# A two-layer hybrid transformer on one core: the first projections fed by adaLN sums in another order, with unread products, split sums and a fixed order of three engines

## The chip, the cores and the metric

The kernel runs on one core of one Trainium2 chip. A core has a matrix engine (TensorE, "PE"; its weight loads are listed as "PEld"), a vector engine (VectorE, "DVE"), a scalar engine (ScalarE, "ACT"), a general engine (GpSimd, "POOL") and a queue engine (SyncE, "SP") that here only issues DMAs. Each engine works through its own queue in order and waits there for semaphores. The metric is the device time of one execution in microseconds (us), the median of several runs.

## The reference

Two residual blocks on a latent sequence `x` (256 x 1024) and a context `ctx` (256 x 1024). Layer 0 mixes by a chunked retention, layer 1 by neighbourhood attention; each is followed by an MLP. What matters here is the start of layer 0: six modulation vectors from one matrix product with `silu(c)` ("ada"), the affine of x and ctx with the first two, and the projection of the result.

```python
silu_c = jax.nn.silu(c)
silu_cc = jax.nn.silu(c_ctx)
for i in range(DEPTH):
    mod = (silu_c @ ada_w[i] + ada_b[i])[:, None, :]
    mod_c = silu_cc @ ada_w[i] + ada_b[i]
    sh1, sc1, g1, sh2, sc2, g2 = jnp.split(mod, 6, axis=-1)
    sh1c, sc1c, g1c, sh2c, sc2c, g2c = jnp.split(mod_c, 6, axis=-1)

    h = x * (1.0 + sc1) + sh1
    hc = ctx * (1.0 + sc1c) + sh1c
    if i % N_MIXERS == 0:
        y, yc = retention_mixer(h, hc, ret_w_in[j], ret_w_o[j], ret_decay[j],
                                ang_row, ang_col, not last)
    ...
    x = layer_norm(DN_ALPHA * x + g1 * y, ln_g[i, 0], ln_b[i, 0])
    ...
```

In the retention mixer `p = h @ w_in` gives q, k, v and a gate for four heads; q and k have 256 columns a head, v and the gate 512.

## The kernel before

**Products in two parts.** All large products are made from float32 values that are split in a high part (rounded to TensorE's fp32r format) and a low part (the difference). `split` makes the high part on ACT and the low part on DVE; `mm3` makes a product from three passes: high by high, high by low, low by high. Activations for the projections stand transposed in `hTh` and `hTl`: eight chunks of 128 features by 512 tokens (256 latent, then 256 context).

**Weights.** `specs` lists all weight blocks in the order of use. `fetch` loads one (`raw`, four buffers), ACT makes `hi`, DVE makes `lo` (five buffers each); `take` hands out the next blocks and fetches ahead.

**The first quarters.** Head 0's q (256 columns) and v (512 columns) are accumulated over eight chunks in six PSUM banks, `pq` (two) and `pv` (four), while ada arrives. The work goes in four quarters of 256 features. `quarter_loads` loads for a quarter ada's columns of the shift (s = 0) and of the scale (s = 1), each in two blocks of 512 rows (`kh`), and then the quarter's columns of x and ctx into `RR`. `quarter_rows` makes ada's sums: `ada_mm` puts 128 columns in each of four 32-row strips of one bank, per input chunk k four small products; `ada_row` adds the bias rows `brows` and stores the row; `ada_columns` turns the row into columns with a product by `sel` and writes `mods[0, 0]` (adding 1 to the scale). `chunk` transposes a feature chunk of x and ctx into one bank; `modulate_chunk` applies the affine, DVE to the latent half and ACT to the context half, and splits the result. `quarter_q` and `quarter_v` are the products, 6 and 12 passes a chunk, so 36 a quarter. `quarter_weights` takes the quarter's two weight blocks.

**The start.** `crow` gathers c, c_ctx and the four norms' rows ln_g and ln_b; one transpose turns them into columns, from which `scol` (silu), `cT` (silu repeated, the stationary operand of ada's sums) and `lnT` come. `lns` is a scaled copy of the norm rows in DRAM, which the layer norms read much later. `cst` holds the constants: identity, `sel`, rotation tables.

**Order.** `InOrder` wraps each engine; where `.on` is set, the instructions of this engine keep the order of the program, else a planner orders them at build time by priority and estimated time. Before, SP is in program order through the quarters, TensorE is ordered by the planner, and ACT and DVE are in program order only around `make_strip`, which makes the four decay strips from exponentials of `dt` (`strip_tables`): none in quarter 0, strip 0 in quarter 1, strip 1 in quarter 2, strips 2 and 3 in quarter 3.

**Behind the quarters.** x and ctx are scaled by ALPHA; head 0's q is rotated (`rotate`, from `pq`), v is copied and split (`evac_v`, from `pv`), k is projected (`proj_T`), then come the gates, the masked scores and the outputs. In the background (`bg`) the rest of ada streams in (`rawa`) and is weighed on DVE.

Of the kernel before, what the change touches and what calls it, by code (L numbers as in the profile page):

```python
# [17 lines left out]
P = 128  # L18
# [21 lines left out]
def make_consts():  # L40
# [14 lines left out]
    add("sel", sel)  # L55
    inv = f(1.0) / (f(10000.0) ** (np.arange(0, 128, 2, dtype=f) / f(128.0)))
# [8 lines left out]
    add("pad", np.zeros((P, -sum(q.shape[1] for q in parts) % LINE)))  # L65
# [39 lines left out]
def kernel(  # L105
# [169 lines left out]

    def lows(n=100):
# [14 lines left out]
    cst = cpool.tile([P, CONSTS.shape[1]], F32, tag="cst", name="cst")  # L291
# [3 lines left out]
    sp.dma_start(out=cst[:], in_=consts)  # L295
    act.dma_start(out=crow[16:48, :], in_=ln_g.rearrange("l i (k p) -> (l i k) p", p=P))
    act.dma_start(out=crow[48:80, :], in_=ln_b.rearrange("l i (k p) -> (l i k) p", p=P))

    def cv(name, p0=0, p1=P):
        o, w = CONST_COLS[name]  # L300
        return cst[p0:p1, o : o + w]
# [6 lines left out]
    pc = bank("pc")  # L308
    pe.transpose(pc[:, 0:80], crow[0:80, :], ident[0:80, 0:80])
    act.activation(out=scol[:].rearrange("p a k -> p (a k)"), in_=pc[:, 0:16], func=AF.Silu)  # L310
    for t in range(2):
        dve.tensor_copy(
            out=cT[:, :, :, t], in_=scol[:, t, :].unsqueeze(2).broadcast_to([P, KC, 16])
        )
    dve.tensor_copy(out=lnT[:].rearrange("p a b c k -> p (a b c k)"), in_=pc[:, 16:80])


    lns = dram.tile([64, P], F32, tag="lns", name="lns")
    lsc = scr("lsc")
    pool.tensor_scalar_mul(out=lsc[0:80, :P], in0=crow[0:80, :], scalar1=ALPHA)  # L320
    act.dma_start(out=lns[:], in_=lsc[16:80, :P])

    mhalf = small(cpool, 1, "mhalf", name="mhalf")
    dve.memset(mhalf[:], -0.5)

    onecol = small(cpool, 33, "onecol", name="onecol")
    lgn = cpool.tile([P, 2, 8], F32, tag="lgn", name="lgn")
    lgm = small(cpool, 4, "lgm", name="lgm")
# [60 lines left out]
    def ada_quarter_load(i, ss):  # L389

        raws = []
        for kh in range(2):
            raw = slot(ss[kh], [P, 2, 4, 256], F32, "rawq")
            for s in range(2):
                w_ap = ada_w[0][512 * kh : 512 * kh + 512, s * D + 256 * i : s * D + 256 * i + 256]
                sp.dma_start(out=raw[:, s], in_=w_ap.rearrange("(k p) n -> p k n", p=P))
            raws.append(raw)
# [291 lines left out]
    pv = [bank("pv") for _ in range(4)]  # L689
    AQ = ((S_GS, S_SH), (S_SL, S_VH))  # L690

    def quarter_loads(i):
        raws = ada_quarter_load(i, AQ[i % 2])
        for a, src in enumerate((x, ctx_in)):
            cols = slice(256 * i, 256 * i + 256)
            sp.dma_start(out=RR[a][:, :, cols], in_=src[0][:, cols].rearrange("(t p) c -> p t c", p=P))
        return raws

    def quarter_ada(pr, raws, kh):
        for k in range(4 * kh, 4 * kh + 4):  # L700
            ada_mm(pr, k, P, lambda j: raws[kh][:, j // 2, k - 4 * kh, (j % 2) * P : (j % 2 + 1) * P])
# [45 lines left out]
    raws = quarter_loads(0)  # L747
    brows = slot(S_T1, [P, 4, P], F32, "brows")
    for j in range(4):
        act.dma_start(  # L750
            out=brows[32 * j : 32 * j + 32],
            in_=bass.AP(
                ada_b.tensor,
                ada_b.offset + (j // 2) * D + (j % 2) * P,
                [[0, 32], [256, 4], [1, P]],
            ),
        )
    def quarter_rows(i, raws):
        pr = bank("pada")
        for kh in range(2):  # L760
            quarter_ada(pr, raws, kh)
        return pr, ada_row(pr, brows[:, i], P)

    def quarter_weights(i):
        return take(1, 2)[0], take(1, 1 if i < 3 else WB)[0]
# [7 lines left out]

    def modulate_chunk(k, pt):
        m = mods[0, 0]
        tmp = scr("aff")
        dve.tensor_scalar(
# [26 lines left out]
    for i in range(4):  # L804
# [16 lines left out]
        if i < 3:  # L821
            wq, wv = wnext
# [1046 lines left out]
```

## Time and profile before

| | us |
|---|---|
| median of three runs | 1231.76 (1231.55 to 1233.69) |
| the profiled execution | 1231.76 |
| its span, first to last instruction | 1230.0 |

All waits within the first 130 us that are above 5 us, by engine and what it waited for: DVE's `row` for TensorE's `pada` 24.7 us in four waits; ACT's `aff` for DVE's `aff` 21.6 us in five; ACT's `hi` for the weights' DMA 13.1 us in three. TensorE itself waited 5.0 us for the first rows of `crow` and 3.3 us for `rawq`.

How to read the rows: in the timeline a row has the start, the length, the engine, the line (a helper records every operation here, so all have the same line and are told apart by their tiles), the operation, out<-in, the count that was merged, and in brackets the idle time before it and what ended it. A float32 matmul stands as two records; a transpose as one. In the table of stretches the columns are the stretch, its length, the busy time and number of instructions of PE, PEld, DVE, ACT and POOL, the granted TensorE clock, the busy share of the DMA engines and GB/s.

### The profile page before, as it was taken

The page shows a single profiled execution, that of the slowest core. Times are in us where ns is not written, and L with a number is a line of the kernel's source. Part 1 is how long each engine was busy: PE and PEld are TensorE (multiplying, and loading weights), DVE is VectorE, ACT ScalarE, POOL GpSimd, SP SyncE. Part 2 cuts the span into 40 slices and gives each one's busy share as a digit, 9 for nine tenths or more (in the row PEclk, how much of TensorE's full clock was granted, in tenths as well). Part 3 has the DMA queues.
Part 4 walks back from the last instruction along what each step waited for, and adds up shares of the span by engine and source line. Part 5 has one row for each costly group of instructions (what it writes and reads, how often), then busy time and mean ns, then how long its engine had stood idle before and what let it go on. Part 6 is the DMA issues. An engine that isn't in the chain of part 4 may idle for free.

```text
span 1230.0 us, 17924 instructions
## 1 busy us (share of the span) xinstructions
PE 1198.3 (97%) x7069; PEld 1000.7 (81%) x7069; DVE 809.0 (66%) x1256; ACT 477.5 (39%) x795; POOL 167.4 (14%) x198
## 2 busy tenths in 40 slices
PE   6999999999999999999999999999999989999996
PEld 4777888888888888888888888788887867999885
DVE  2597857777585476667766664467575678776445
ACT  2462232323223245442113341146465565655340
POOL 2004401420340140000120000131111110000001
PEclk9999999999999999999999999999999999999998
DMA  9665443375543224326656656336345643565660
GB/s 310 224 210 193 142 133 107 120 245 124 149 154 105 75 69 138 111 90 205 197 164 213 193 182 215 126 87 184 88 138 158 187 140 108 179 211 187 223 206 35
DMA packets 140516, 194.53 MB, mean 158 GB/s; under 512 B 22440, under 2 KB 84112, under 8 KB 140432
## 3 DMA queue, kind: packets, MB, share of 16 engines
q1 hardware_dynamic: 135440, 180.86, 46.4%
q0 software_dynamic: 3264, 9.46, 3.0%
q10 hardware_dynamic: 1728, 3.07, 0.8%
q8 instruction: 55, 0.90, 0.3%
q14 instruction: 29, 0.24, 0.1%
HBM read 188.53 MB, written 5.75 MB: 158 GB/s over the span
## 4 chain that ended last, share of the span: by engine, by line
PE 85%; DVE 6%; ACT 4%; DMA 2%; issue 1%; POOL 1%; SPq 0%; DVEq 0%; POOLq 0%; ACTq 0%
PE p L84 41%; PE pq L84 7%; PE pv L84 7%; PE pw L84 6%; PE pg L84 6%; PE pn L84 4%; PE pnv L84 3%; PE pada L84 2%; PE po L84 2%; ACT s L84 2%; DVE lo L84 1%; DMA rawa<-in_ada_w_dram 1%; PE pnw L84 1%; PE ppt L84 1%; PE pS L84 1%
## 5 line engine op out<-in xcount | busy, mean ns | idle before, releaser
L84 DVE TENSOR_TENSOR lo<-raw,hi 128x1024 fp32r<-128x1024 f32 (+1 forms) x228 | 277.2, 1226 | 158.5 <-ACT hi L84 158.4
L84 ACT CAST hi<-raw 128x1024 fp32r<-128x1024 f32 (+1 forms) x228 | 234.1, 1036 | 353.5 <-PE p L84 183.5
L84 PE MATMUL p<-hi,hid 128*128 128x512 f32 (+1 forms) x832 | 242.4, 374 | 0.0
L84 PEld LDWEIGHTS p<-hi,hid 128*128 128x128 f32 x832 | 152.2, 188 | 28.7 <-issue 1.2
L84 PE MATMUL p<-hTh,lo 128*128 128x256 f32 (+1 forms) x512 | 169.6, 331 | 0.8 <-DVE lo L84 0.8
L84 PE MATMUL p<-hTh,hi 128*128 128x256 f32 (+1 forms) x512 | 169.9, 332 | 0.0
L84 PE MATMUL p<-hTl,hi 128*128 128x256 f32 (+1 forms) x512 | 169.3, 331 | 0.0
L84 PE MATMUL p<-lo,hid 128*128 128x512 f32 (+1 forms) x416 | 155.3, 373 | 0.0
L84 POOL TENSOR_TENSOR R<-R,acc 128x512 f32<-128x512 f32 x40 | 65.9, 1657 | 298.9 <-DVE acc L84 298.7
L84 PEld LDWEIGHTS p<-hTh,lo 128*128 128x128 f32 x512 | 98.0, 191 | 9.7 <-DVE lo L84 1.0
L84 PEld LDWEIGHTS p<-hTh,hi 128*128 128x128 f32 x512 | 98.0, 191 | 9.5 <-issue 0.8
L84 PEld LDWEIGHTS p<-hTl,hi 128*128 128x128 f32 x512 | 98.0, 191 | 8.7
L84 DVE SCALAR_TENSOR_TENSOR acc<-rawa,scol,acc 128x1024 f32<-128x1024 f32 x49 | 62.2, 1282 | 46.7 <-DMA rawa<-in_ada_w_dram 46.6
L84 PEld LDWEIGHTS p<-lo,hid 128*128 128x128 f32 x416 | 78.4, 188 | 13.5
L84 DVE SCALAR_TENSOR_TENSOR strips<-rawa,scol,strips 128x512 f32<-128x512 f32 x84 | 70.0, 885 | 4.0 <-DMA rawa<-in_ada_w_dram 4.0
L84 ACT CAST hid<-r 128x256 fp32r<-128x256 f32 (+1 forms) x64 | 32.0, 500 | 83.6 <-DVE r L84 83.6
L84 POOL TENSOR_SCALAR rstd<-mv 128x1 f32<-128x1 f32 x28 | 10.5, 376 | 366.7 <-DVE mv L84 366.7
L84 ACT ACTIVATE s<-s,mn 128x512 f32<-128x512 f32 x64 | 45.5, 712 | 32.3 <-DVE mn L84 32.3
L84 DVE TENSOR_TENSOR hid<-r,hid 128x256 fp32r<-128x256 f32 (+1 forms) x64 | 34.6, 541 | 29.5 <-ACT hid L84 29.4
L84 PE MATMUL pq<-hTh,hi 128*128 128x512 f32 x128 | 50.4, 397 | 1.8 <-ACT hTh L84 1.8
L84 PE MATMUL pw<-hi,oh 128*128 128x512 f32 x128 | 51.2, 400 | 0.0
L84 PE MATMUL pg<-hi,hTh 128*128 128x512 f32 x128 | 51.0, 398 | 0.0
(191 smaller groups left out, 2248.0 us busy)
## 6 DMA issues: line engine op xcount, KB each, us to landing
raw<-in_mlp_w_dram SPq DMA_DIRECT2D x128, 512.0 KB
rawa<-in_ada_w_dram SPq DMA_DIRECT2D x80, 512.0 KB
raw<-in_ret_w_in_dram SPq DMA_DIRECT2D x46, 512.0 KB
raw<-in_nat_w_in_dram SPq DMA_DIRECT2D x24, 512.0 KB
rawq<-in_ada_w_dram SPq DMA_DIRECT2D x16, 512.0 KB
raw<-in_ret_w_o_dram SPq DMA_DIRECT2D x16, 512.0 KB
bias<-rpb_rows POOLq DMA_DIRECT2D x16, 256.0 KB, 4.2
raw<-in_nat_w_o_dram SPq DMA_DIRECT2D x8, 512.0 KB
```

The source lines that it names most:

```text
L84: r = f(*args, **kwargs)
```

## The change

**Start.** The constants are loaded in two parts: `cst0` (identity, `sel` and a new `sel2`, 140 columns) at once, the rest in quarter 0. `crow` gathers c, c_ctx and ada's bias for the first two vectors; the norm rows come in quarter 1 (`ln_rows`, on ACT's queue), their transpose, `lnT` and `lns` in quarter 3 (`ln_columns`; `lns` goes from ACT's queue to POOL's). `brows` and its four DMAs are gone: the bias stands in columns (`bcol`, with the 1 of the scale) and is added where `mods` is written.

**Loads.** x's and ctx's first quarter goes on ACT's queue, later ones on SP's ahead of ada's blocks. The blocks come in the order s = 0 (both `kh`), then s = 1. The first two weight blocks are loaded ahead of the second quarter; `load` leaves the making of their parts to two functions, `high` and `low`, which are called one chunk at a time.

**Order.** From `first_columns` to the end of the quarters ACT, DVE and TensorE keep the program's order.

**Sums.** `quarter_sums` makes the sums of one s from 16 matmuls of 128 columns: even and odd input chunks in different strips, which `sel2` adds up when the row becomes columns. Their number for a quarter stays (32).

**First quarter.** The transposes of chunks 0 and 1, by kind (latent, context) into two banks each, stand between the third and the fourth ada block; 4, 3 and 6 short products of a constant tile (`turn_over`), whose result nothing reads, stand ahead of the last sums, between them and the columns, and behind the columns. `modulate_kinds` writes the high part of each kind straight from PSUM (ACT latent, DVE context), then the other way round a full copy, and the low part as the difference. `first_products` orders the 18 passes of chunk 0 by the parts as they come.

**Later quarters.** The sums stand in halves between v's products of the quarter before; the second half of the sums' bank takes the context's transposes. `modulate_chunk` now makes the high part on DVE and the full copy on ACT. The ALPHA scaling and three weight blocks come ahead of quarter 3's last products.

```diff
+    def load():
+        src, k, ncol = specs[len(units)]
+        raw = rawp.tile([P, k, ncol], F32, tag="raw", name=nm("raw"))
+        sp.dma_start(out=raw[:], in_=src.rearrange("(k p) n -> p k n", p=P))
+        ...
+        def high(i):
+            act.copy(out=hi[:, i], in_=raw[:, i])
+        def low(i):
+            dve.tensor_sub(out=lo[:, i], in0=raw[:, i], in1=hi[:, i].bitcast(F32))
+        return high, low
...
-    sp.dma_start(out=cst[:], in_=consts)
-    act.dma_start(out=crow[16:48, :], in_=ln_g.rearrange("l i (k p) -> (l i k) p", p=P))
-    act.dma_start(out=crow[48:80, :], in_=ln_b.rearrange("l i (k p) -> (l i k) p", p=P))
+    act.dma_start(out=crow[16:32, :], in_=ada_b[0][0 : 2 * D].rearrange("(r p) -> r p", p=P))
+    act.dma_start(out=cst0[:], in_=consts[:, 0:NC0])
...
+    def ln_rows():
+        rows = scr("rows")[:, :P]
+        act.dma_start(out=rows[0:32, :], in_=ln_g.rearrange("l i (k p) -> (l i k) p", p=P))
+        act.dma_start(out=rows[32:64, :], in_=ln_b.rearrange("l i (k p) -> (l i k) p", p=P))
+        return rows
...
+    def turn_over(n):
+        for _ in range(n):
+            pe.matmul(pq[0][:, :256], lhsT=still[:, :P], rhs=still[:, :256], start=True, stop=True)
...
+    def quarter_sums(pr, raws, s, ks):
+        for k in ks:
+            lhsT = cT[:, k, :, :].rearrange("p a t -> p (a t)")
+            for half in range(2):
+                j = 2 * (k % 2) + half
+                pe.matmul(
+                    pr[32 * j : 32 * j + 32, tsl(s)],
+                    lhsT=lhsT,
+                    rhs=raws[k // 4][:, s, k % 4, tsl(half)],
+                    ...
+    def quarter_columns(pr, row, c0):
+        for s in range(2):
+            pe.matmul(
+                pr[:, 4 * s : 4 * s + 4], lhsT=row[:, tsl(s)], rhs=cv("sel2"), start=True, stop=True
+            )
+        dve.tensor_add(out=mods[0, 0][:, :, c0 : c0 + 2, :], ...
...
     def modulate_chunk(k, pt):
...
-        split(tmp[:], hTh[:, k, :], hTl[:, k, :])
+        tmp = scr("aff")
+        for e, dst in ((dve, hTh[:, k, :]), (act, tmp)):
+            for a in range(2):
+                modulated(e, dst[:, KINDS[a]], pt[:, KINDS[a]], k, a)
+        dve.tensor_sub(out=hTl[:, k, :], in0=tmp[:], in1=hTh[:, k, :].bitcast(F32))
+
+    def modulate_kinds(k, pts, between=lambda: None):
+        tmp = scr("aff")
+        for e, a in ((act, 0), (dve, 1)):
+            modulated(e, hTh[:, k, KINDS[a]], pts[a], k, a)
+        between()
+        for e, a in ((act, 1), (dve, 0)):
+            modulated(e, tmp[:, KINDS[a]], pts[a], k, a)
+        dve.tensor_sub(out=hTl[:, k, :], in0=tmp[:], in1=hTh[:, k, :].bitcast(F32))
...
+    quarter_x(0, act)
+    raws = ada_quarter_load(0, AQ[0])
+    wq_parts, wv_parts = load(), load()
+    raws1 = quarter_loads(1)
+    for e in (act, dve, pe):
+        e.on = True
+    pr = bank("pada")
+    first_columns()
+    quarter_sums(pr, raws, 0, range(KC))
+    quarter_sums(pr, raws, 1, range(0, 4))
+    pts = [chunk_kinds(k) for k in range(2)]
+    turn_over(4)
+    quarter_sums(pr, raws, 1, range(4, KC))
+    row = quarter_row(pr)
+    turn_over(3)
+    quarter_columns(pr, row, 0)
+    turn_over(6)
+    (qhigh, qlow), (vhigh, vlow) = wq_parts, wv_parts
+    qhigh(0)
+    modulate_kinds(0, pts[0], lambda: qlow(0))
+    vhigh(0)
+    vlow(0)
+    qhigh(1)
+    modulate_kinds(1, pts[1])
+    qlow(1)
+    vhigh(1)
+    vlow(1)
...
     for i in range(4):
         k = 2 * i
-        quarter_q(k, 0, wq)
+        wq, wv = take(2, 0)
         if i < 3:
-            pr, row = quarter_rows(i + 1, raws)
-        quarter_v(k, 0, wv)
+            wq_parts, wv_parts = load(), load()
+        if i == 0:
+            tabs = strip_tables()
+            sp.dma_start(out=cst1[:], in_=consts[:, NC0:])
+        if i < 2:
+            raws2 = quarter_loads(i + 2)
+        if i == 0:
+            first_products(wq, wv)
+        else:
+            quarter_q(k, 0, wq)
+            modulate_chunk(k + 1, chunk(k + 1))
+            quarter_v(k, 0, wv)
...
         quarter_q(k + 1, 1, wq)
+        if i == 3:
+            ln_columns(rows)
+            take(0, 3)
+            for a in range(2):
+                dve.tensor_scalar_mul(out=RR[a][:], in0=RR[a][:], scalar1=ALPHA)
+            quarter_v(k + 1, 1, wv)
+        else:
+            pr = bank("pada")
+            quarter_sums(pr, raws, 0, range(KC))
+            quarter_v(k + 1, 1, wv, range(2))
+            if i:
+                both(wv_parts)
+            pts = chunk_kinds(k + 2, pr)
+            quarter_sums(pr, raws, 1, range(KC))
+            row = quarter_row(pr)
+            quarter_v(k + 1, 1, wv, (2,))
+            quarter_columns(pr, row, k + 2)
+            modulate_kinds(k + 2, pts)
+            quarter_v(k + 1, 1, wv, (3,))
+            if i == 0:
+                both(wv_parts)
+            if i == 1:
+                rows = ln_rows()
+            raws = raws2
         for h in ((), (0,), (1,), (2, 3))[i]:
             make_strip(h, *tabs)
-        act.on = dve.on = False
+    act.on = dve.on = False
```

More of the change, by code (lines that the diff above doesn't have):

```diff
@@ L64, in make_consts @@
         add("sin" + nm, np.sin(ang) * sg)
-    add("pad", np.zeros((P, -sum(q.shape[1] for q in parts) % LINE)))
     base = np.concatenate(parts, axis=1)
@@ new lines, in both @@
+    def both(parts):
+        for k in range(2):
+            for f in parts:
+                f(k)
+    quarter_x(0, act)
[11 more added lines that the diff above has]
+    quarter_sums(pr, raws, 1, range(4, KC))
```

170 lines of the change are left out of this document (94 added, 76 removed).

## The prediction, made before any run of the changed kernel

> **What bounds the kernel now.** I read the page first, then busy time by stretches, then the timeline of the first 80 us, because the change lies there.
>
> ```profile
> span 1230.0 us, 17924 instructions
> PE 1198.3 (97%) x7069; PEld 1000.7 (81%) x7069; DVE 809.0 (66%) x1256; ACT 477.5 (39%) x795; POOL 167.4 (14%) x198
> ```
> ```profile
> 6.00:18.60 12.60, 7.35 (x74) 4.99 (x74) 2.23 (x8) 2.18 (x5) 0.00 (x0) 1.00 1.09 339
> 62.00:70.00 8.00, 8.00 (x36) 6.50 (x36) 7.86 (x14) 8.00 (x15) 0.00 (x0) 1.00 0.63 211
> ```
>
> TensorE has work in 97% of the span, so the time is TensorE's queue plus its gaps. The stretch from 6 to 18.6 us is the largest gap: TensorE is busy for 7.35 of 12.60 us while the DMA engines are full (share 1.09, 339 GB/s). The profiled execution is itself the median run, 1231.76 us: its span of 1230.0 and 1.76 around it. My sum is made against that.
>
> The head, before the first product, reads so:
>
> ```profile
> 1.35 0.33 ACTq L84 DMA_DIRECT2D crow<-in_ln_g_dram  x1
> 1.61 3.63 SPq L84 DMA_DIRECT2D rawq<-in_ada_w_dram  x4
> 1.71 0.43 ACTq L84 DMA_DIRECT2D crow<-in_ln_b_dram  x1
> ...
> 11.23 0.19 PEld L84 LDWEIGHTS pada<-rawq,cT 128*32 128x32 f32 x4 [0.58 <-DMA rawq<-in_ada_w_dram]
> ...
> 12.70 1.92 PE L84 MATMUL pada<-rawq,cT 128*32 128x128 f32 x28 [0.83 <-DMA rawq<-in_ada_w_dram]
> 14.56 1.12 PE L84 MATMUL pt<-cst,R 128*128 128x128 f32 x4
> 14.67 0.29 DVE L84 TENSOR_TENSOR row<-pada,brows 128x128 f32<-128x128 f32 x1 [8.56 <-PE pada L84]
> ...
> 15.46 0.43 PE L84 MATMUL pada<-cst,row 128*128 128x8 f32 x2
> ...
> 15.94 0.23 DVE L84 TENSOR_SCALAR mod<-pada 128x4 f32<-128x4 f32 x2 [0.97 <-PE pada L84]
> ...
> 17.04 1.02 ACT L84 ACTIVATE aff<-pt,mod 128x256 f32<-128x256 f32 x2 [1.43 <-DVE aff L84]
> ...
> 17.95 0.61 ACT L84 CAST hTh<-aff 128x512 fp32r<-128x512 f32 x1
> 18.59 0.69 DVE L84 TENSOR_TENSOR hTl<-aff,hTh 128x512 fp32r<-128x512 f32 x1 [0.54 <-ACT hTh L84]
> 18.61 1.22 PE L84 MATMUL pq<-hTh,hi 128*128 128x512 f32 x2 [1.77 <-ACT hTh L84]
> ...
> 20.49 0.63 PE L84 MATMUL pq<-hTl,hi 128*128 128x512 f32 x1
> 20.92 0.63 PE L84 MATMUL pq<-hTh,lo 128*128 128x512 f32 x1
> ...
> 22.73 0.39 PE L84 MATMUL pv<-lo,hTh 128*128 128x512 f32 x1
> 22.96 0.40 PE L84 MATMUL pv<-hi,hTl 128*128 128x512 f32 x1
> ```
>
> Behind ada's last block (landed at 12.70) stands a serial chain: sums, row, columns, mod, the affine on DVE, then on ACT (which waited for DVE, not beside it), the cast, the first product at 18.61. That product starts at half pace: 0.43 us from start to start (20.49 to 20.92), and only 0.23 from 22.73 on.
>
> From there TensorE runs without a gap, in four quarters:
>
> ```profile
> 33.24 0.39 PE L84 MATMUL pq<-hTh,hi 128*128 128x512 f32 x1
> ...
> 46.10 0.39 PE L84 MATMUL pq<-hTh,hi 128*128 128x512 f32 x1
> ...
> 47.23 0.39 PE L84 MATMUL pq<-hTh,lo 128*128 128x512 f32 x1
> 47.55 1.08 PE L84 MATMUL pada<-rawq,cT 128*32 128x128 f32 x32
> 48.56 0.50 PE L84 MATMUL pv<-hi,hTh 128*128 128x512 f32 x1
> ...
> 55.22 0.60 PE L84 MATMUL pt<-cst,R 128*128 128x128 f32 x4
> 55.58 0.48 PE L84 MATMUL pv<-hi,hTh 128*128 128x512 f32 x1
> ...
> 58.43 0.39 PE L84 MATMUL pq<-hTh,hi 128*128 128x512 f32 x1
> ...
> 66.65 0.39 PE L84 MATMUL pq<-hTh,hi 128*128 128x512 f32 x1
> ```
>
> The quarters last 14.63 (from 18.61), 12.86, 12.33 and 8.22 us. The last holds nothing but 36 products, 0.228 each (8.2). A group of 32 ada records between products costs 48.56 - 47.23 - 0.23 = 1.10; four transposes cost 0.36.
>
> **The head, part by part.** *Blocks.* Ahead of the fourth block went its 2048 KB, constants and bias rows; now x's and ctx's quarter (512 KB) come on ACT's queue beside the blocks, the bias shrinks to 8 KB, half of the constants go later.
>
> ```profile
> rawq<-in_ada_w_dram SPq DMA_DIRECT2D x16, 512.0 KB
> R<-in_x_dram SPq DMA_DIRECT2D x4, 256.0 KB
> brows<-in_ada_b_dram ACTq DMA_DIRECT2D x4, 64.0 KB
> cst<-in_consts_dram SPq DMA_DIRECT2D x1, 136.0 KB
> ```
>
> That is 2440 KB before, some 2630 after: 0.6 us more at 339 GB/s. Against it SP issues its four blocks sooner: they took it 3.63 us, with single issues of ACT at 0.33 to 0.43. I take the third block at 10.5 (11.23 before), with 9.5 and 11.3 as ends, the fourth at 12. [...]
>
> *TensorE to the first product.* At the slow pace a transpose or a group of four ada records takes 0.21 (four transposes: 1.12 with their tail, as at 14.56; the pace of 28 records at 12.70 is the same). The unread products are not in the trace; half of a 512-wide one at half pace is 0.21, at full pace 0.11, and I take the slow one. From 10.5: 16 records 0.85, eight transposes 1.7, four unread products 0.85, 16 records 0.85, to 14.75. The fourth block is then no longer waited for. Row (0.29 for 128 columns; 0.3 to 0.5 for 256, taken 0.4) with its signal to 15.3, columns (two matmuls for one, 0.65) to 15.95, one add to 16.25. ACT and DVE now take one kind each from two banks and write the high part itself: 0.55 (two took 1.02), to 16.85. TensorE's six unread products run from 15.85 to 17.1. So the first product is at 17.1 (16.0 to 18.0): **-1.5 us**. The bias adds, the silu and the weight casts lie under the waits for blocks; the first weights follow the fourth block by 0.75 us and are split by then.
>
> **The quarters.** First: 8.2 for 36 products, two groups of sums 2.2, one set of transposes 0.36, columns 0.45, together 11.2. The clock: from 18.61 to the full pace took nearly 4 us (by 22.73); now unread products begin at 13, so I give it 1.4 us of half pace, which costs 0.7 (ends 0 and 1.9). And a wait at the boundary: behind the second group come row (0.55 with signals), three products, columns, add, high part (0.55), and only three products lie over add and high part: 0.3 us. Sum 12.2 against 14.63: **-2.4**.
>
> Second and third: two sets of transposes, the same groups, and at the start a wait of 0.37 for the low part (both other halves 0.55 and the difference 0.69 against four products of 0.9): 12.2 each. At the end of the second quarter, ln_g's and ln_b's rows are issued on ACT (0.33 + 0.43) ahead of strip 0's four exponentials. Behind these on ACT's and DVE's now fixed order stands the odd chunk's high part, 0.8 late (0 to 0.8). The two come to 25.2 against 25.19: **0**. The splits of weights gain nothing, since TensorE did not wait for them.
>
> Last: the odd chunk's transposes have moved here (0.36), ln's transpose 0.15, the low part's wait 0.37: 9.05 against 8.22: **+0.8**. So the quarters end at 63.5, 3.1 us earlier.
>
> **Behind the quarters.** What is late next is DVE. Its fixed order now has three low parts, two scalings and strips 2 and 3 ahead of head 0's rotation:
>
> ```profile
> 55.64 1.23 DVE L84 TENSOR_SCALAR R<-R 128x2048 f32<-128x2048 f32 x1 [0.29 <-PE pt L84]
> ...
> 57.38 2.35 DVE L84 TENSOR_TENSOR lo<-raw,hi 128x1024 fp32r<-128x1024 f32 x2
> ...
> 69.76 0.36 DVE L84 TENSOR_SCALAR strips<-e 128x384 f32<-128x384 f32 x1
> ...
> 72.80 0.36 DVE L84 TENSOR_SCALAR strips<-e 128x384 f32<-128x384 f32 x1
> ...
> 77.66 1.88 DVE L84 TENSOR_TENSOR vl<-pv,vh 128x512 fp32r<-128x512 f32 x3
> ...
> 81.72 1.29 DVE L84 TENSOR_TENSOR t<-pq,cst 128x256 f32<-128x256 f32 x3
> ```
>
> From the last chunk's low part at 60.0: lows 3.6, scalings 2.5, two strips at some 2.5 (five operations, nearly 3.0 from end to end at 69.76 and 72.80 with others between) to 71.3; eight rotations of 0.43 and signals to 75.2; four of v's lows to 77.8; the next weight's low to 79. TensorE is through K at 63.5 + 12.6 = 76.1 (48 products of 0.228 and three groups of ada records beside them) and wants that weight six products later, at 77.8. A wait of 1.2 if the order stays so, none if the planner puts the low first: I take **+0.5**. After that nothing of the change remains but one transfer of lns from POOL's queue, read much later.
>
> Sum: -1.5 - 2.4 + 0 + 0.8 + 0.5 = -2.6, and 1231.76 - 2.6 = 1229.2 us.
>
> **The rivals.** *A, the head gives more.* Block three lands at 9.5 (-1.0), the clock is up at the first product (-0.7), no wait behind the quarters (-0.5): 1227.0. For it: ln's rows and the four bias loads no longer go ahead of the blocks. Against it: 512 KB more go beside them.
>
> *B, the unread products do not raise the clock.* Then it comes up some 3.7 us after the first product as before (from 18.61 to between 20.92 and 22.73), which loses 1.85 for 0.7: 1230.4. For it: ada's sums and eight transposes ran almost without a gap from 12.70 to 16.8 and the products at 18.61 were slow all the same. Against it: the new ones are whole 128 x 128 products. [...]
>
> *C, DVE becomes the bound of head 0, and the kernel is slower.* If the planner leaves that weight's low behind K's rotation too, it comes at 77.8 + 3.9 + 1.2 = 83.0, and TensorE at 77.8 waits 5.2: 1231.76 - 3.1 + 5.2 = 1233.9. It decides as soon as the give-back exceeds 3.1. For it: DVE is busy for 7.86 of 8 us from 62 to 70 already, and the change takes nothing off it. Against it: no wait of TensorE on DVE stands there now.
>
> **How the numbers follow.** Forecast 0.42, A 0.20, B 0.13, C 0.25. About 0.2% (2.46 us, hence 1229.3) can be told from no change. The forecast's own range, 1228 to 1230.6, lies across that mark: 0.24 of it faster, 0.18 the same; A is faster; B gives 0.03 faster and 0.10 same; C gives 0.20 slower and 0.05 same. So faster 0.47, same 0.33, slower 0.20. The range reaches from under A, with the boundary waits gone as well, to C: 1226.3 to 1234.0.
>
> **What would show it.** First product at 17.1 and not waiting for a DMA; its successors 0.23 apart from about 18.5; boundaries at 29.3, 41 to 42, 54, and K's first product near 63.5. A TensorE row waiting for DVE lo between 76 and 84 shows C. Wrong would be: products above 0.4 apart after 20, a wait on rawq in a later quarter, or ACT held by lgn's landing when the second chunk's columns are ready.

## The result, and the profile after

The changed kernel takes 1234.14 us, the median of 20 runs (1231.8 to 1236.0); the kernel before took 1231.42 on the same chip (20 runs, 1229.45 to 1233.88). The ratio of the runs is 1.0016, with a 95% interval of 1.0010 to 1.0022: slower by 2.0 us (the medians lie 2.7 apart). The profiled run of after took 1235.42 us, 1.3 above its median, so the two profiles lie 3.6 us apart, and the losses read from them add up to more than 2.0. Its page begins:

```profile
span 1233.6 us, 17994 instructions
PE 1200.1 (97%) x7091; PEld 1001.2 (81%) x7091; DVE 816.5 (66%) x1271; ACT 477.7 (39%) x803; POOL 167.9 (14%) x199
```

TensorE's timeline of after answers to the starts that the prediction named (start, length, engine, operation, tiles, idle time before and what ended it):

```profile
16.03 0.95 PE L89 MATMUL pq<-still 128*128 128x256 f32 x6
17.11 0.70 PE L89 MATMUL pq<-hTh,hi 128*128 128x512 f32 x2
17.64 0.62 PE L89 MATMUL pq<-hTh,lo 128*128 128x512 f32 x2
...
29.22 0.70 PE L89 MATMUL pq<-hTh,hi 128*128 128x512 f32 x2
...
41.51 0.40 PE L89 MATMUL pv<-hi,hTl 128*128 128x512 f32 x1
42.04 0.70 PE L89 MATMUL pq<-hTh,hi 128*128 128x512 f32 x2
42.57 0.62 PE L89 MATMUL pq<-hTh,lo 128*128 128x512 f32 x2
43.34 0.74 PE L89 MATMUL pq<-hTl,hi 128*128 128x512 f32 x2
...
49.07 0.73 PE L89 MATMUL pq<-hTl,hi 128*128 128x512 f32 x2 [0.67 <-DVE hTl L89]
...
56.03 0.70 PE L89 MATMUL pq<-hTh,hi 128*128 128x512 f32 x2
...
62.56 0.73 PE L89 MATMUL pq<-hTl,hi 128*128 128x512 f32 x2 [0.40 <-DVE hTl L89]
...
66.30 0.39 PE L89 MATMUL pq<-hTh,hi 128*128 128x512 f32 x1
...
82.44 0.64 PE L89 MATMUL pada<-rawa,cT 128*32 128x256 f32 x8 [1.84 <-DMA rawa<-in_ada_w_dram]
...
126.62 0.66 PE L89 MATMUL pT<-cst,gs 128*128 128x128 f32 x4 [1.57 <-POOL gs L89]
```

The first product comes at 17.11, the second pair of products 0.53 behind it: the head and the first quarter took the forecast time (12.11 us to 29.22). The later quarters last 12.82, 13.99 and 10.27 us, and K's first product stands at 66.30, only 0.35 before the 66.65 of the kernel before. Two losses follow that before does not have: the wait for `rawa` at 82.44 and the wait for `pT` at 126.62.

**What the quarters lost.** The starts of TensorE's records, from the first product to K's first, give this sum (us). Each record is charged the time to the next start; of a product with more than 0.40 to the next start, 0.23 is product and the rest is wait.

| | before | forecast | after |
|---|---|---|---|
| 144 products | 35.7 | 32.8 | 36.0 |
| ada's sums | 7.9 | 6.6 | 6.1 |
| transposes and columns | 2.7 | 3.7 | 3.9 |
| half pace at the start | 1.7 | 0.7 | 0 |
| waits | 0 | 2.8 | 3.2 |
| together | 48.0 | 46.6 | 49.2 |

The forecast's column holds its own terms; rounded by quarters they gave 46.45. The change does save on the sums (1.9) and on the half pace (1.7), but it buys waits that before does not have (3.2) and more transposes and columns (1.2). The products cost what they cost before. The forecast took 0.228 for each, the pace of the last quarter of before, which holds nothing else; in every other quarter, before and after, some products start 0.30 to 0.34 after the one ahead of them, and the average is 0.25. What makes these slow was not tested.

At 42.04 and 43.34 a product starts 0.3 later than the 0.23 from one product to the next would have it (41.51 to 42.04; two products at 42.57, then 43.34): TensorE waits for `hTh` and then for `hTl`, some 1.8 us over the three boundaries. The marked waits at 49.07 and 62.56 come from the odd chunk and cost 0.83 and 0.56 from start to start. ACT's and DVE's rows for it, in after:

```profile
46.16 1.00 DVE L89 TENSOR_SCALAR hTh<-pt,mod 128x256 fp32r<-128x256 f32 x2
47.27 1.02 ACT L89 ACTIVATE aff<-pt,mod 128x256 f32<-128x256 f32 x2 [2.01 <-DVE hTh L89]
48.32 0.69 DVE L89 TENSOR_TENSOR hTl<-aff,hTh 128x512 fp32r<-128x512 f32 x1 [1.17 <-ACT aff L89]
```

ACT's full copy begins only when both of DVE's high parts are done: 1.0, then 1.0, then 0.7, one behind the other. Both engines read the same bank, and ACT waits for DVE 2.01 us here and 1.99 us at the next odd chunk. Whether the bank is the cause this profile does not show; the run with two banks, below, bears on it.

**What the raw buffers lost.** DVE behind the quarters, and SP's queue, both of after:

```profile
63.53 0.22 DVE L89 COPY lnT<-pc 128x64 f32<-128x64 f32 x1 [1.03 <-PE pc L89]
63.68 3.48 DVE L89 TENSOR_TENSOR lo<-raw,hi 128x1024 fp32r<-128x1024 f32 x3
67.08 2.35 DVE L89 TENSOR_SCALAR R<-R 128x2048 f32<-128x2048 f32 x2
```
```profile
49.80 15.48 SPq L89 DMA_DIRECT2D raw<-in_ret_w_in_dram  x3
66.06 1.48 SPq L89 DMA_DIRECT2D rawa<-in_ada_w_dram  x2
76.45 0.38 SPq L89 DMA_DIRECT2D raw<-in_ret_w_in_dram  x1
78.84 4.63 SPq L89 DMA_DIRECT2D rawa<-in_ada_w_dram  x2
```

and SP's queue of before:

```profile
43.58 16.55 SPq L84 DMA_DIRECT2D raw<-in_ret_w_in_dram  x5
61.35 0.34 SPq L84 DMA_DIRECT2D rawa<-in_ada_w_dram  x1
...
68.22 0.38 SPq L84 DMA_DIRECT2D raw<-in_ret_w_in_dram  x1
74.83 4.78 SPq L84 DMA_DIRECT2D rawa<-in_ada_w_dram  x2
```

The three low parts of K's blocks start at 63.68, where the planner of before had the first two at 57.38. A `raw` buffer is free only when its low part is made, and ada's streamed blocks use the same four buffers. So the last load of the group of three goes out at 64.9 (49.80 + 15.48 - 0.37; before 59.8), right behind the first of the three low parts, and ada's first streamed block at 66.06 (61.35), behind the second. The next weight block, at 76.45 (68.22), and ada's third block, at 78.84 (74.83), then find only buffers that the first two streamed blocks still hold: SP waits 5.7 and 1.9 us for TensorE's sums of these blocks (from 75.76 and from 78.14, 0.64 us each). TensorE wants the third block at 80.6 and gets it at 82.44. Right behind this wait the granted clock fell, as the table of stretches of after shows (length, busy time and count of PE, PEld, DVE, ACT, POOL, then the clock):

```profile
83.10:86.50 3.40, 3.40 (x8) 2.70 (x9) 3.34 (x8) 0.00 (x0) 0.00 (x0) 0.50 0.61 180
```

Half the clock for 3.4 us is another 1.7 us in this profile, an estimate: eight products take 3.53 us there (starts at 83.01 and 86.54), where at the 0.23 of those behind them (86.54 to 86.77) they would take 1.84. That half clock makes the changed kernel slower is not shown: the granted clock averages 0.9958 over its 20 runs and 0.9951 over the 110 runs of before that stand beside the experiments, so before loses more to half clock in all. From K's first product to the first of the scores (`pS`) after needs 23.07 us (66.30 to 89.37), before 19.71 (66.65 to 86.36).

**What w_o lost.** At 126.62 the chain is this, in after:

```profile
123.13 1.05 ACT L89 CAST hi<-raw 128x1024 fp32r<-128x1024 f32 x1 [5.04 <-DMA raw<-in_ret_w_o_dram]
...
124.56 1.09 ACT L89 ACTIVATE sg<-pg 128x512 f32<-128x512 f32 x2
```
```profile
125.23 2.57 POOL L89 TENSOR_TENSOR gs<-sg,gs 128x512 f32<-128x512 f32 x2 [7.89 <-ACT sg L89]
```

ACT waits for a block of w_o with `sg` behind it; `sg` feeds `gs`, `gs` feeds the transposes. In before this block's high part was made at 117.14, six us earlier. After this wait the two kernels keep their distance: 4.4 us at 248 us (247.71 before, 252.10 after), 3.6 at the end of the two profiles. Before has a stretch at half clock near 470 us that after has not, which takes 1.4 off; around 1020 to 1036 each has one, and 0.5 comes back there. The row near 470 in the table of stretches of before:

```profile
469.50:472.80 3.30, 3.23 (x15) 3.23 (x16) 3.12 (x8) 2.77 (x6) 0.00 (x0) 0.50 0.55 156
```

### The profile page after: what moved, and what is told of

Read it like the earlier page. It is cut to its first block, busy times and chain, and to the rows that moved or that the text cites. A ratio compares the mean times of both kernels' runs of the same rounds, so it can differ in the third digit from the quotient of the medians.

```text
span 1233.6 us, 17994 instructions
## 1 busy us (share of the span) xinstructions
PE 1200.1 (97%) x7091; PEld 1001.2 (81%) x7091; DVE 816.5 (66%) x1271; ACT 477.7 (39%) x803; POOL 167.9 (14%) x199
## 4 chain that ended last, share of the span: by engine, by line
PE 82%; DVE 7%; ACT 4%; DMA 3%; issue 2%; POOL 1%; SPq 1%; ACTq 0%; DVEq 0%; POOLq 0%
PE p L89 40%; PE pq L89 6%; PE pw L89 6%; PE pg L89 6%; PE pv L89 6%; PE pn L89 4%; PE pnv L89 3%; PE po L89 2%; PE pada L89 2%; ACT s L89 2%; PE pS L89 1%; DVE lo L89 1%; PE ppt L89 1%; DMA raw<-in_ret_w_in_dram 1%; ACT hi L89 1%
## 5 line engine op out<-in xcount | busy, mean ns | idle before, releaser
L89 PE MATMUL pg<-lo,hTh 128*128 128x512 f32 x128 | 50.9, 397 | 0.0
```

Of the source, the lines that this page charges most:

```text
L89: r = f(*args, **kwargs)
```

## The experiments

Each was timed in five rounds beside the kernel before, which took 1231.2 to 1232.1 us (medians of the five groups of runs); so the ratios to it are compared. All start from the changed kernel. "Quarters" is the time from the first product to K's first, "to pS" from there to the scores; in the free order K's products mix with the last quarter's, so it has no such split.

| kernel | us | ratio, 95% interval | first product | quarters | to pS | largest waits of TensorE behind it |
|---|---|---|---|---|---|---|
| before | 1231.42 | 1 | 18.61 | 48.04 | 19.71 | none above 0.5 |
| changed | 1234.14 | 1.0016 (1.0010 to 1.0022) | 17.11 | 49.19 | 23.07 | rawa 1.8, pT 1.6 |
| splits early | 1232.09 | 0.9996 (0.9986 to 1.0007) | 16.26 | 49.15 | 20.55 | rawa 0.9, pT 1.3 |
| odd in two banks | 1233.59 | 1.0013 (1.0004 to 1.0023) | 17.37 | 47.89 | 22.05 | rawa 1.9, pT 1.7 |
| free order | 1231.06 | 0.9996 (0.9985 to 1.0007) | 17.29 | | | pT 1.7 |
| no unread products | 1236.92 | 1.0042 (1.0026 to 1.0058) | 14.71 | 51.82 | 22.11 | rawa 2.1, row 1.6, pT 1.6 |
| both | 1230.57 | 0.9992 (0.9981 to 1.0003) | 16.43 | 47.84 | 20.16 | pT 1.3 |
| strips inside | 1231.55 | 0.9997 (0.9988 to 1.0005) | 16.23 | 50.57 | 20.62 | row 1.7 |
| weighing first | 1230.41 | 0.9992 (0.9983 to 1.0001) | 15.66 | 50.65 | 20.90 | row 1.7 |
| fast head | 1230.38 | 0.9990 (0.9980 to 1.0001) | 15.59 | 50.28 | 20.28 | ol 0.8, hTl 0.6 |
| v's tiles moved | 1229.08 | 0.9981 (0.9972 to 0.9989) | 16.10 | 46.41 | 20.35 | pT 1.3 |
| weighing pinned | 1236.00 | 1.0041 (1.0026 to 1.0056) | 16.02 | 46.74 | 20.41 | strips 2.2, lo 1.3 |
| strips spread | 1228.09 | 0.9970 (0.9959 to 0.9981) | 16.05 | 47.72 | 19.50 | row 1.1 and 0.8 |
| row first | 1227.94 | 0.9969 (0.9958 to 0.9979) | 15.99 | 47.23 | 19.89 | row 0.8 and 0.4 |

**Splits early.** Two of K's blocks get their parts in the third quarter.

```diff
             if i:
                 both(wv_parts)
+            if i == 2:
+                take(0, 4)
             pts = chunk_kinds(k + 2, pr)
```

> Two of the three weight blocks of K are split a quarter earlier (high and low part in the second half of the third quarter, where DVE idles 2.9 us ahead of row). Theory (late low parts hold the raw buffers, so ada's third streamed block is issued late, TensorE waits 1.84 us for it at 82.4 and drops to half clock): the next K block's raw load is issued near 52.5 instead of 64.9, TensorE's wait for rawa near 82 falls below 0.5 us, no half-clock window there, pS starts near 86 instead of 89.4, and the wait for pT near 126 shrinks too; time 1229.5 to 1231. Rival (the loss is half-clock windows that fall anywhere, or the unread products and the extra records): time stays at 1233.5 to 1234.5.

SP's queue of this run:

```profile
48.95 2.72 SPq L89 DMA_DIRECT2D raw<-in_ret_w_in_dram  x3
52.44 11.95 SPq L89 DMA_DIRECT2D rawa<-in_ada_w_dram  x2
```

The third weight load goes out at 51.3 instead of 64.9, ada's first streamed block at 52.44 instead of 66.06, and no stretch at half clock follows. The way to `pS` is 2.52 us shorter, the ratio falls by 0.0020. The theory holds in place and for most of the size; but a wait of 0.9 for `rawa` (below 0.5 was expected) and one of 1.3 for `pT` stay, and the time, 1232.09, misses the range of 1229.5 to 1231.

**Odd chunk in two banks.**

```diff
-            modulate_chunk(k + 1, chunk(k + 1))
+            modulate_kinds(k + 1, chunk_kinds(k + 1))
```

> The odd chunk of each quarter is transposed into two banks and modulated one kind per engine, as the even one. Theory (ACT waits for DVE because both read one bank): ACT's aff no longer waits 2 us for DVE's hTh; TensorE's waits for hTl at 49 (0.67) and 62.6 (0.40) go, K's first product at about 65.0 instead of 66.3. The transfer that TensorE waits for at 82.4 moves by at most 1 us with DVE, so the time falls by 0.3 to 1.0: 1233.1 to 1233.8. Rival (the bank is not the cause, strips ahead on DVE are): ACT still waits over 1 us and K's first product stays within 0.3 of 66.3, time 1234.

ACT's rows for the last two odd chunks, and TensorE's largest wait, in this run:

```profile
47.06 0.56 ACT L89 ACTIVATE aff<-pt,mod 128x256 f32<-128x256 f32 x1 [1.08 <-DVE hTh L89]
...
59.88 0.56 ACT L89 ACTIVATE aff<-pt,mod 128x256 f32<-128x256 f32 x1 [1.02 <-DVE hTh L89]
```
```profile
81.51 0.64 PE L89 MATMUL pada<-rawa,cT 128*32 128x256 f32 x8 [1.94 <-DMA rawa<-in_ada_w_dram]
```

ACT's wait is halved, not gone: on two banks it still waits 1.08 and 1.02 us for DVE's first half when the two change sides. That is enough. (The edit changes the division of the work along with the banks, so it does not separate the two; that ACT waits only where it turns to DVE's bank speaks for the bank.) The quarters are 1.30 us shorter, but the streamed block stops TensorE for 1.94 all the same, and the ratio moves by 0.0003 (0.4 us, as the theory had it): too little for this measurement to tell from nothing. A gain in front of another wait is hardly one.

**Free order.** ACT, DVE and TensorE are in program order only for the first products, and ACT and DVE around the strips.

```diff
+    act.on = dve.on = pe.on = False
     for i in range(4):
...
+        act.on = dve.on = True
         for h in ((), (0,), (1,), (2, 3))[i]:
             make_strip(h, *tabs)
+        act.on = dve.on = False
```

> ACT, DVE and TensorE keep the program's order only up to the first products and around the strips, as before; all else of the change stays. Theory: the planner puts the low parts of K's blocks ahead again, their raw buffers come free before 60, no wait for rawa near 82: 1230 to 1232. Rival (the order costs nothing, the added waits at the boundaries do): 1233.5 to 1234.5, K's first product not before 66.

DVE in this run, around the last boundary:

```profile
54.02 0.42 DVE L89 COPY row<-pada 128x256 f32<-128x256 f32 x1 [3.19 <-PE pada L89]
54.36 1.22 DVE L89 TENSOR_TENSOR lo<-raw,hi 128x1024 fp32r<-128x1024 f32 x1
55.50 0.16 DVE L89 TENSOR_TENSOR mod<-pada,bcol 128x8 f32<-128x8 f32 x1
```

The planner puts K's low parts back between the chunk's own steps, ada's streamed blocks go out at 57.4, the wait near 82 is gone, and the time is within the expected range. It is the fixed order, not the loads or the sums, that held the buffers; which of the three engines' orders did it was not separated.

**No unread products.** The three calls of `turn_over` are left out.

> The 13 unread products are left out. Theory (they bring the clock up at 14.8): the first product comes at 16.9 to 17.1, the half pace lasts to about 20 to 22, the second quarter starts 1.0 to 2.0 us later (30.2 to 31.2 instead of 29.2), and since DVE, not TensorE, is what is late at 82 half of it is hidden: 1234.3 to 1235.8. Rival (the sums and transposes alone keep the clock up): second quarter at 29.2, time 1234 or a little below.

TensorE's head in this run, and the same rows of the changed kernel:

```profile
10.90 1.14 PE L89 MATMUL pt<-cst,R 128*128 128x128 f32 x8
11.98 0.64 PE L89 MATMUL pada<-rawq,cT 128*32 128x128 f32 x16
```
```profile
11.24 1.97 PE L89 MATMUL pt<-cst,R 128*128 128x128 f32 x8
...
14.00 1.01 PE L89 MATMUL pada<-rawq,cT 128*32 128x128 f32 x16
```

A stretch at half clock, and ahead of it ACT's row for the decay and TensorE's wait, in this run:

```profile
28.10:31.50 3.40, 3.40 (x9) 2.19 (x9) 3.17 (x5) 2.04 (x4) 3.27 (x3) 0.50 1.10 349
```
```profile
25.13 0.21 ACT L89 ACTIVATE lgn<-lgn 128x8 f32<-128x8 f32 x1 [5.46 <-DMA lgn<-in_ret_decay_dram]
```
```profile
27.14 0.61 PE L89 MATMUL pada<-cst,row 128*128 128x4 f32 x4 [1.58 <-DVE row L89]
```

Both theories missed. The first product comes 2.4 us earlier without any unread product, and the products behind it run at full pace (four in 0.90 us from 18.19 on). Part of that is TensorE's pace ahead of it: eight transposes take 1.14 us here and 1.97 in the changed kernel, the 16 records of the sums behind them 0.64 and 1.01. (The changed kernel's clock record starts at 14.80, at full; ahead of that the clock column shows 1.00 whatever the pace, so the rows above are the evidence.) So the unread products are not needed for full pace. Fast head, below, has none either, with the first product at 15.59; v's tiles moved has them, with 16.10. What they cost at the same clock is not shown.

The second quarter starts at 28.68, 0.54 earlier only. On ACT's fixed order the exponential of the decay stands ahead of the weights' high parts, it waits 5.46 us for its load, DVE's low parts wait for the high parts, and `row` stands behind those. TensorE then waits 1.58 and runs 3.4 us at half clock. The median of the five runs is 2.8 us above the changed kernel's, the profiled run (1235.81) only 0.4. The granted clock averages 0.9942 over the five runs against 0.9958, which is some 2 us of lost clock (an estimate, 0.0016 of 1234); where in the other runs it was lost stays open.

**Both.** The early splits and the two banks together.

> The two edits together: odd chunk in two banks, and two of K's blocks split a quarter earlier. Theory (two separate losses, one in the quarters, one in the raw buffers): from the first product to K's first product 47.8 us instead of 49.2, pS another 0.8 to 1.3 us earlier than with the early splits alone, time 0.7 to 1.3 below the early splits alone: 1230.8 to 1231.4. Rival (the streamed block of ada still sets the end, so quarters that end earlier only wait longer for rawa): pS as before the second edit, a wait for rawa above 1.5 us, time 1232.

Quarters as expected (47.84), and from the first product to `pS` 68.00 us against 69.70 with the early splits alone; ratio 0.9992. Once the streamed block is no longer late, the 1.3 us of the banks reach `pS` in the profile. The time, 1230.57, lies just under the expected range, and the ratio cannot be told from that of the early splits alone (0.9996).

**Strips inside.** `both`, and the strips are made behind the odd chunk: 0 and 1 in the second quarter, 2 in the third, 3 in the fourth.

> As the two edits together, and the strips are made inside the quarters (0 and 1 in the second, 2 in the third, 3 in the fourth, behind the odd chunk) instead of behind them. Theory (DVE's queue behind the quarters sets when raw buffers and ada's blocks move): DVE has 2.5 to 5 us less behind K's first product, the wait for rawa near 84 falls below 0.3, the wait for pT near 122 (1.3) stays because its cause lies elsewhere; time 0.3 to 1.0 below the two edits: 1230.0 to 1231.0. Rival: strips inside the quarters delay rows or low parts there and K's first product comes later, time not below.

A miss (1231.55 us, above the range): two strips are too much for the second quarter. DVE's `row` comes 1.70 late at 41.63, and the clock is at half from 43.8:

```profile
43.80:47.20 3.40, 3.40 (x12) 2.39 (x11) 1.23 (x3) 0.56 (x1) 0.00 (x0) 0.50 0.66 198
```

Unexpectedly the wait for `pT` is gone: the planner's order behind the quarters had changed with it.

**Weighing first.** As strips inside, and one background step stands between gs of tokens 1 and 2.

> As the one before, with one background step moved so that DVE weighs the last streamed block of part one ahead of gs for tokens 2 and 3. Theory (the third block of w_o waits for a raw buffer that DVE's weighing holds; its high part stands ahead of sg on ACT, sg feeds gs, gs feeds pT): that block is issued near 112 to 113.5 instead of 115.6, TensorE's wait for pT near 122 falls from 1.3 to below 0.3, time 0.8 to 1.4 below the one before: 1229.0 to 1230.0. Rival (the wait comes from ACT's or POOL's own order): wait stays over 1.0, time unchanged.

The `pT` wait had gone already, so this run does not tell its theories apart; `row` is 1.68 late again.

**Fast head.** As weighing first, without the unread products, and the second quarter's q weights are split behind `row`.

> As the one before, without the 13 unread products, and the second quarter's q weights are split behind row instead of ahead of it, where row stood behind a load. Theory A (DMA, full to 45 us, sets the quarters): first product near 14.7, but TensorE waits for rawq or raw in the first three quarters and K's first product comes within 0.7 us of the one before; with half clock somewhere in the quarters the time is 0 to 2 us above it. Theory B (the quarters are TensorE's): K's first product 1.5 to 2.4 earlier, time 1.5 to 2.4 below.

K's first product comes at 65.87, 0.44 earlier than in the run before it, and the ratio is 0.9990 against 0.9992: in place and time that is theory A, not B. But A's cause is not shown: no wait of TensorE for `rawq` or `raw` stands in the first three quarters. What stands there are 0.55 for `row` and 0.93 for `hTh` in the head, half clock behind them (16.1 to 19.5 us), and later 0.45 for `row` and 0.36 and 0.56 for `hTl`. The first product, at 15.59, is later than the 14.7 of A. Here the unread products neither cost nor earn what the time could tell.

**v's tiles moved.** As both, and v's four token tiles at a quarter's end are dealt out otherwise.

```diff
-            quarter_v(k + 1, 1, wv, range(2))
+            quarter_v(k + 1, 1, wv, (0,))
...
             row = quarter_row(pr)
-            quarter_v(k + 1, 1, wv, (2,))
+            quarter_v(k + 1, 1, wv, (1,))
             quarter_columns(pr, row, k + 2)
             modulate_kinds(k + 2, pts)
-            quarter_v(k + 1, 1, wv, (3,))
+            quarter_v(k + 1, 1, wv, (2, 3))
```

> The two edits of the joint run (odd chunk in two banks, two K blocks split a quarter earlier), and v's products at the end of a quarter are dealt out otherwise: token tile 0 ahead of the transposes, tile 1 over row, tiles 2 and 3 over the columns and the high part. Theory (at each boundary three products of 0.23 cover 1.0 us of columns, add and high part, so TensorE waits 0.3 for hTh and as much for hTl): six products cover it, K's first product comes 0.9 to 1.8 earlier after the first product than the 47.84 of the joint run (46.0 to 46.9), time 0.5 to 1.2 below it: 1229.4 to 1230.1, if the wait for rawa near 83 (0.40) does not grow by as much. Rival (a full DMA queue to 45 us sets the boundaries): K's first product within 0.4 of the joint run.

A boundary of this run:

```profile
53.11 0.39 PE L89 MATMUL pv<-hi,hTl 128*128 128x512 f32 x1
53.34 0.62 PE L89 MATMUL pq<-hTh,hi 128*128 128x512 f32 x2
53.80 0.63 PE L89 MATMUL pq<-hTh,lo 128*128 128x512 f32 x2
54.27 0.70 PE L89 MATMUL pq<-hTl,hi 128*128 128x512 f32 x2
```

All starts are 0.23 a product apart: both waits of this boundary are gone, and the quarters take 46.41, as the theory had it (46.0 to 46.9). The time, 1229.08, is 0.3 below its range. The ratio, 0.9981, is the first whose interval lies below 1.

**Weighing pinned.** The weighing of the last streamed blocks is placed ahead of `gs` of tokens 2 and 3 by a fixed order, four background steps at once.

> As the one before, with the weighing of the last streamed blocks of part one placed ahead of gs of tokens 2 and 3 on DVE by a fixed order (part two's first block is loaded earlier by it). Theory (DVE's weighing holds the raw buffer of w_o's third block): that block is issued by 113, TensorE's wait for pT near 121 (1.3) falls below 0.3, time 0.8 to 1.3 below the one before. Rival (a fixed order makes gs wait for weighing, or the block loaded earlier takes the buffer instead): the wait stays over 1.0 or a new one of that size stands before 121.

The rival. DVE now holds the weighing of several blocks in one piece, TensorE waits 2.21 for it, and w_o's last block goes out at 124.9, later than in any other profile; the wait for `pT` is gone, but one of 1.3 for w_o's low part takes its place:

```profile
106.71 9.35 DVE L89 SCALAR_TENSOR_TENSOR strips<-rawa,scol,strips 128x512 f32<-128x512 f32 x14
```
```profile
115.55 0.63 PE L89 MATMUL pada<-strips,misc 128*32 128x256 f32 x4 [2.21 <-DVE strips L89]
```

Of the 5.4 us between this profile and that of v's tiles moved, 2.9 stand at 140 us, where the same TensorE records are compared; the rest comes far behind and stays open.

**Strips spread.** As v's tiles moved, and strip 0 is made inside the second quarter, 1 inside the third, 2 behind it, 3 inside the fourth.

> As the run with v's tiles moved, with the strips one place earlier: strip 0 inside the second quarter, 1 inside the third, 2 behind the third, 3 inside the fourth. DVE has one strip (2.6 us) less behind the quarters, and in the order that the planner then makes all weighing of the last streamed block stands ahead of gs of tokens 2 and 3. Theory (that weighing holds the raw buffer of w_o's third block): the block is issued near 110 to 112, the wait for pT near 120 (1.32) falls below 0.3, row in the second quarter not late by more than 0.3; time 0.7 to 1.4 below that run: 1227.7 to 1228.4. Rival (the wait has another cause): it stays over 1.0 and the time at 1229.

SP's loads of w_o in this run, and in the run with v's tiles moved:

```profile
96.03 14.57 SPq L89 DMA_DIRECT2D raw<-in_ret_w_o_dram  x3
```
```profile
96.91 16.37 SPq L89 DMA_DIRECT2D raw<-in_ret_w_o_dram  x3
```

The last of the three goes out at 110.2 (96.03 + 14.57 - 0.37) instead of 112.9, and the wait for `pT` is gone. DVE's order decides it: here the last weighing of a streamed block starts at 108.80, ahead of `gs` at 110.97, and the load goes out 1.4 later; there the weighing stands between and behind the two `gs`, the last of it starting at 112.15, and the load goes out 0.8 after that. The profiles agree: in before, in strips inside, weighing first, fast head, strips spread and row first the weighing stands ahead of `gs` and no wait for `pT` of 1.0 follows; in the changed kernel and in six runs (splits early, odd in two banks, free order, no unread products, both, v's tiles moved) it ends behind the first `gs` and the wait is 1.3 to 1.7. This is agreement over thirteen profiles, not an edit of that order alone; the one such edit, weighing pinned, brought other waits. `row` is late by more than the 0.3 expected, 1.05 and 0.81, and the time is in the expected range all the same.

**Row first.** As strips spread, and the second quarter's q weights are split behind `row`.

> As the strips run, and the split of the second quarter's q weights stands behind row on ACT's and DVE's fixed order. There ACT waited 4.27 us for the decay's landing (25.28) before it could make those high parts, DVE's low parts waited for these, and row behind them came 1.05 us late for TensorE. Theory: row is on time, the wait before the columns near 27 falls below 0.2, the second quarter starts 12.0 to 12.4 after the first product instead of 13.17, and 0.5 to 1.1 of it stays in the time: 1227.0 to 1227.6. Rival (the loads, full to 45 us, set the second quarter's end): it starts earlier but the third does not, time within 0.4 of the strips run.

The wait of 1.05 at 27 is gone and the second quarter starts 11.84 behind the first product; of these 1.3 us, 0.5 are left at the third quarter's start (24.86 against 25.37) and 0.1 at `pS` (67.12 against 67.22): TensorE waits again, 0.4 for the third quarter's `row` and 0.3 for `rawa`. The theory holds in place, but its gain does not reach the time: 1227.94 us against 1228.09, not to be told apart, and above the expected 1227.0 to 1227.6. These two beat both kernels: 0.31% under before.

## Why the prediction was wrong

It said 1229.2 us and faster; the result is 1234.14 and slower, just outside the range. Step by step:

- *Head, -1.5 us:* right in size, 17.11 against 17.1, and by luck. The same head gave first products from 15.66 to 17.37 in the other ten profiles that kept the unread products, and in three of them and in the changed kernel they follow TensorE's pace ahead of them: busy throughout from 12.0 to 14.8 us, it had 34 records there where the first product came at 15.66 (weighing first), 29 at 16.23 (strips inside), 26 at 17.11 (the changed kernel) and 23 at 17.37 (odd in two banks). The sum's slow pace up to some 14.75 happened to fit this one profile, whose clock record starts at 14.80. That the unread products raise the clock is not shown: in no unread products the sums ran at 16 records in 0.64 us from 11.98 on, against 1.01 from 14.00 on here.
- *First quarter, -2.4:* right, 12.11 against 12.2, but with errors that cancel: the half pace (0.7) did not come, and the products took 0.7 more than the 8.2 they were given.
- *Second and third quarter, 0:* **a step that failed.** 26.81 against 25.2. The term that was mis-sized is the products: 8.2 us for 36, a pace read from a quarter without sums and transposes; they took 8.95 and 9.30. The waits fit in sum, 2.03 against 2.14, but one of them for a wrong reason: 0.8 was set aside for the odd chunk behind ln's rows, and ACT never waited for these; it waited 2.0 us for DVE on the shared bank, which cost TensorE 0.83. With two banks the quarters are 1.30 us shorter.
- *Last quarter, +0.8:* 10.27 against 9.05: products 8.85 instead of 8.2, and a wait of 0.56 at the odd chunk that the sum put at nothing. With the banks and v's tiles put right the quarters take 46.41, close to the forecast's 46.45 (12.2 + 25.2 + 9.05), but that is chance: the forecast had 3.5 us of waits and half pace in it, and there under 1 is left.
- *Behind the quarters, +0.5 (0 to 1.2):* **the step that failed most.** It read DVE's queue for the next weight's low part on TensorE's path. What came late instead were raw buffers: low parts 6 us later, ada's block 4 us later, TensorE 1.84 us idle and then, in this profile, at half clock: +3.4 at `pS`, and 2.5 of it gone with two low parts moved. "After that nothing of the change remains" was wrong as well: the planner's other order of DVE near 112 us goes with 1.4 more.
- *Rivals:* C had place and sign (TensorE waiting between 76 and 84) and by chance the price, 1233.9, but not the mechanism: TensorE waits for no low part there. B's late clock did not come, and A's early one came without A's gain behind the quarters.
- *Signs:* of those that it named, products more than 0.4 apart after 20 us came (0.53 at each boundary, 1.06 at 48.01). TensorE did not wait for `rawq` in a later quarter, and ACT's wait for `lgn` (2.26 us) ended at 24.33, four us ahead of the columns.

## What to carry to other kernels

Take the pace of products from a stretch with the same neighbours: 0.228 us a product in a quarter of products alone became 0.25 among sums and transposes, 3.2 us over 144. When low parts, copies or sums are moved later on an engine that is not the bound, list which buffers they hold and which load waits for these, until the load meets the engine that is the bound; here 6 us on DVE became 1.84 us on TensorE 19 us later. Give two engines that are to work side by side on one tile a bank each: here that, with the work divided by kind, brought ACT's wait from 2.01 to 1.08 us and took 1.30 us off the quarters. A fixed order is paid where it puts an instruction that waits for a load ahead of one on the path, and it shifts the planner's order far behind it: compare both orders, also where nothing was edited.

## What the hardware showed unexpectedly

In the first 130 us, short waits of TensorE were followed by a stretch of 3.4 us at half clock in five places: after waits of 1.84 us (the changed kernel, 82.4), 1.70 and 1.68 (strips inside and weighing first, near 41), 1.58 (no unread products, 27.1), and 0.55 and 0.93 close together (fast head, 14 to 15.6). After others of 1.94 (odd in two banks, up to 81.51; the clock was 1.00 from 83.1 to 86.5) and 2.21 (weighing pinned, up to 115.55; the products at 117.66 and 117.97 are 0.31 apart) none followed, nor after the 1.57 for `pT` in the changed kernel (1.00 from 126.6 to 135). No unread products has 0.55 and 0.93 in its head as well (ahead of 13.17 and 14.71), and the clock was 1.00 from 14.8 to 19.5. So length alone does not decide.

In the traces of before and of the changed kernel, the changes of the granted clock lie whole multiples of 3.413 us apart: 68.27 us from 14.80 to 83.07 in the changed kernel is 20 of these steps, 447.15 from 22.31 to 469.46 in before is 131. Whether the place of a wait on these steps decides was not shown. Such stretches also stand where nothing was edited: before has one at 469.46 and one at 1032.66 us, the changed kernel one at 1018.32. So a single profile can differ from another by 1.4 us, as by the stretch near 470, for a reason that no edit set.
